# Convolution histories and taps loaded as rows of 32 channels and turned by VectorE; the first norm's scales loaded feature by feature

## The chip, the cores and the metric

The kernel runs on one core of a Trainium2 chip. A core has TensorE (PE; its weight loads are shown apart as PEld), VectorE (DVE), ScalarE (ACT), GpSimd (POOL) and SyncE (SP, which here only issues DMAs), and 16 DMA engines that all queues share. The metric is the device time of one execution in microseconds. The kernel before took 1661.09 us, the median of three runs (1659.3 to 1661.68).

## What is computed

One layer of a hybrid decoder for 256 new positions (the prompt) and 8 sequences of 4 positions (the samples), which continue from stored states. Cut to what bears on the change:

```python
proj = x @ w_in                                    # x: 288 rows of 2048 features
gB, gC, h, q, k, v, z, b_logit, a_logit, m_a, m_b = jnp.split(proj, split_points, axis=-1)
# convolutions along time, one per channel; the samples start from the last rows of their history
conv_out, new_conv_a = causal_depthwise_conv(gC * h, conv_a_buf, conv_a_w)            # 1024 channels, 3 taps, 2 rows
qkv, new_gdn_buf = causal_depthwise_conv(concat([q, k, v], -1), gdn_buf, gdn_conv_w)  # 3072 channels, 4 taps, 3 rows
...
o, S = gated_delta_rule(qh, kh, vh, g, beta, S0)
o = o * lax.rsqrt(jnp.mean(o * o, -1, keepdims=True) + NORM_EPS) * gdn_norm_w
...
x = layer_norm(ALPHA * x + merged @ w_o, ln1_g, ln1_b)
x = layer_norm(ALPHA * x + jnp.square(relu(x @ w_up)) @ w_down, ln2_g, ln2_b)
```

The inputs that the change concerns are the two histories (`state_gdn_conv`: 8 x 3 rows of 3072 channels; `state_conv_a`: 8 x 2 rows of 1024), the taps (`gdn_conv_w`: 4 rows of 3072; `conv_a_w`: 3 rows of 1024), the scales of the first layer norm (`ln1_g`, `ln1_b`: 2048 values each) and `gdn_norm_w` (128 values). In memory the channels are the fast index; the kernel wants channels on the 128 partitions.

## The kernel before

**Tiling.** Features stand on partitions, the 288 positions along the free dimension. Every large product runs over weight blocks of 512 KB, numbered from 0 in the order of the list `blocks`. Block i is loaded by SP into one of four buffers `raw` (`load(i)`, L177), split into a high part by ACT (`hi`, L187) and a low remainder by DVE (`lo`, L142), and used by 24 matmuls (L219 with `hi`, L221 with `lo`), which add into a PSUM accumulator `acc`. There are two accumulators, used in turn. A buffer `raw` is free again when DVE has made `lo`.

**The order of the work is written out by hand.** The main loop goes through the blocks; each turn of it puts instructions at the end of the queues of the engines, and each engine works its queue off in that order. Up to block 9 a turn i splits block i + 2 and, at its end, loads block i + 6. What a turn has for PE besides the matmuls stands in the list `fill` and is put between them, one entry after each second `lo` matmul. When a product is complete, its copies out of the accumulator are put into one of the next turns (`due`).

**The first blocks.** Blocks 0 to 3 serve the first two accumulators at once; blocks 4 to 7 finish them in turn, block 6 the first and block 7 the second. Block 8 begins the third product in the first accumulator, so it waits until turn 7's `conv_evac` (`pair`) has copied the first accumulator out (L277 and L279, ACT, two feature tiles). These copies go into the padded rows `w`, on which the convolution over time is done: ACT puts the samples' history in front (L278, from `hw`) and multiplies by the first tap (L281), DVE adds the other taps (L145).

**Histories and taps.** `hw` holds, for the 24 feature tiles of q, k and v, 24 columns of history and 4 of taps; `hwa` holds the same for the 8 tiles of the other convolution (16 and 3). `lnp` holds the scales of the first norm and `gdn_norm_w`. Before, SP loads the rows as they stand in memory into `hwr`, `har` and `lnr` (seven DMAs, behind the load of block 5). In turn 6 the entries `hist_tiles` and `hist_tiles2` of `fill` turn them by eleven PE transposes (L999, L1006 to L1008), and ACT copies the results out of PSUM (L1000, L1009, L1010, L1012). `gdn_norm_w` is used first when z is processed, `ln1_g` and `ln1_b` after that.

**DMAs on SP.** SP's and ACT's DMAs share eight completion semaphores in turn. An issue that takes up a semaphore again waits until the DMA that had it before, eight issues earlier, has landed; SP's later issues wait behind it.

**The middle.** From turn 8 on a generator (`side`) adds the work of the delta rule to the turns. Around turn 50, POOL and ACT copy the parts of `v3` (L1418 and L1416, `v<-hl`), from which ACT spreads `vm` (L1467) head by head.

Of the kernel before, what the change touches and what calls it, by code (L numbers as in the profile page):

```python
# [9 lines left out]
F32 = mybir.dt.float32  # L10
# [6 lines left out]
P = 128  # L17
# [88 lines left out]
def hybrid_kernel(ctx: ExitStack, tc: tile.TileContext, A):  # L106
# [31 lines left out]
    act, dve, pe, gps, sp = nc.scalar, nc.vector, nc.tensor, nc.gpsimd, nc.sync  # L138
# [22 lines left out]
    fill = []  # L161

    def at(i, f):
        due.setdefault(i, []).append(f)


    def load(i, steps=(), between=()):
        if i >= len(blocks):
            return
        gi, r0, k0, _, _ = blocks[i]  # L170
        t = wp.tile([P, KB, GW], F32, tag="raw", name=nm("raw"))
        kb, cols = gi["kb"], gi["cols"]
        dst = t.rearrange("p k c -> p (k c)").rearrange("p (k c) -> p k c", k=kb)
        src = gi["W"][r0:r0 + kb * P, gi["col0"]:gi["col0"] + cols].rearrange("(k p) c -> p k c", p=P)
        k = 0
        for step in steps or (kb,):
            sp.dma_start(dst[:, k:k + step], src[:, k:k + step])  # L177
            k += step
            if between:
                between.pop(0)()  # L180
        raw[i] = t
# [64 lines left out]
    ident = cst("ident")  # L246
# [630 lines left out]
    tx = tx_cm.__enter__()  # L877
# [12 lines left out]
    xsr = A["x_sample"].rearrange("b t (c j p) -> c (b t) j p", j=4, p=P)  # L890

    xtb, xm = (tx.tile([P, 1024], F32, name=n) for n in ("xtb", "xm"))
    hwr = tx.tile([112, 768], F32, name="hwr")
    har = tx.tile([76, 256], F32, name="har")
    lnr = tx.tile([33, P], F32, name="lnr")

    raw[0] = wp.tile([P, KB, GW], F32, tag="raw", name=nm("raw"))

# [3 lines left out]
    def x_sample_in(c, queue=sp):  # L902
        queue.dma_start(xs4[:, c * P:c * P + P], xsr[c])
# [15 lines left out]
    load(3)  # L919
    sp.dma_start(xr[2], xpr[:, :, 1024:1536])  # L920
    x_sample_in(2)
    gps.memset(epsc[:, 0:1], LN_EPS)
    gps.memset(epsc[:, 1:2], NORM_EPS)
    gps.memset(epsc[:, 2:3], 1.28e-10)

    def later_loads():
        sp.dma_start(xr[3], xpr[:, :, 1536:2048])
        x_sample_in(3)
        load(5)
        sp.dma_start(hwr[0:96, :], A["state_gdn_conv"][0].rearrange("b j (g c) -> (b j g) c", g=4))  # L930
        sp.dma_start(hwr[96:112, :], A["gdn_conv_w"][0].rearrange("j (g c) -> (j g) c", g=4))
        sp.dma_start(har[0:64, :], A["state_conv_a"][0].rearrange("b j (g c) -> (b j g) c", g=4))
        sp.dma_start(har[64:76, :], A["conv_a_w"][0].rearrange("j (g c) -> (j g) c", g=4))
        sp.dma_start(lnr[0:16, :], A["ln1_g"].rearrange("o (k p) -> (o k) p", p=P))
        sp.dma_start(lnr[16:32, :], A["ln1_b"].rearrange("o (k p) -> (o k) p", p=P))
        sp.dma_start(lnr[32:33, :], A["gdn_norm_w"])


    def x_sample(i):
# [52 lines left out]
            act.copy(xh[:, ks, 0:NP_], xv)  # L992
            tt(xl[:, ks, 0:NP_], xv, xh[:, ks, 0:NP_], SUB)

    def hist_tiles():
        g = gtile()
        hv = hw.rearrange("p (g u) c -> p u g c", u=6)
        for u in range(4):
            pe.transpose(g[:, u * 112:u * 112 + 112], hwr[:, u * P:(u + 1) * P], ident[0:112, 0:112])  # L999
        act.copy(hv[:, 0:4], g[:, 0:448].rearrange("p (u c g) -> p u g c", u=4, g=4))  # L1000

    def hist_tiles2():
        hv = hw.rearrange("p (g u) c -> p u g c", u=6)
        g2 = gtile()
        for u in range(2):
            pe.transpose(g2[:, u * 112:u * 112 + 112], hwr[:, (4 + u) * P:(5 + u) * P], ident[0:112, 0:112])  # L1006
            pe.transpose(g2[:, 224 + u * 76:300 + u * 76], har[:, u * P:(u + 1) * P], ident[0:76, 0:76])
        pe.transpose(g2[:, 376:409], lnr, ident[0:33, 0:33])  # L1008
        act.copy(hv[:, 4:6], g2[:, 0:224].rearrange("p (u c g) -> p u g c", u=2, g=4))  # L1009
        act.copy(hwa.rearrange("p (g u) c -> p u g c", u=2),  # L1010
                 g2[:, 224:376].rearrange("p (u c g) -> p u g c", u=2, g=4))
        act.copy(lnp, g2[:, 376:409])  # L1012


    G_ = {}
# [604 lines left out]
    idle = lambda: None  # L1620
# [23 lines left out]
    for i in range(len(blocks)):  # L1644
        cur[0] = i
        ahead = AHEAD if i > 9 else 2
        if i == 10:
            split_hi(i + 2)
            split_lo(i + 2)
        if i > 5:  # L1650
            split_hi(i + ahead)
        if i in (1, 3):
            a_, s_, b_ = x_fill(i // 2 + 1)
            fill.extend([idle, a_, s_, b_])
        if i == 5:
            fill.extend([idle, idle, lambda: x_sample(3)()])
        if i == 6:
            fill.extend([idle, idle, idle, idle, hist_tiles, hist_tiles2])
        if i == 7:
            tx_cm.__exit__(None, None, None)  # L1660
            gcm = tc.tile_pool(name="gdn", bufs=1)
            gpool = gcm.__enter__()
            gd["pool"] = gpool
            gd["w1"] = [gpool.tile([P, 640], F32, tag=f"w1{u}", name=f"w1{u}") for u in range(2)]
            for w in gd["w1"]:
                gps.memset(w[:, 0:3], 0.0)
            gps.memset(stBA, 0.0)
            for G in range(2):
                gd["kq", G] = gpool.tile([P, 4, 4, 2, 64], F32, tag="kq", name=f"kq{G}", bufs=2)
                gd["kqs", G] = gpool.tile([P, 2, 4, 8, 4], F32, tag="kqs", name=f"kqs{G}", bufs=2)  # L1670
                gd["v", G] = gpool.tile([P, 2, 4, 2, 64], F32, tag="vf", name=f"vf{G}")
                gd["vs", G] = gpool.tile([P, 4, 8, 4], F32, tag="vfs", name=f"vfs{G}")
        if i > 7 and sgen:
            if i == mark["merge"]:
                for _ in sgen:
                    pass
                sgen = None
            else:
                next(sgen, None)
                if aux and next(aux[0], aux) is aux:  # L1680
                    aux.pop(0)
            if i == mark["z"] + 4:
                states_out(24, 32, 2, 18, "vf", A["new_conv_a_prompt"][0, 0], A["new_conv_a_sample"][0])
            if i == mark["conv"] + 1:
                gd["ao"] = ap_.tile([P, 2, H, NT], F32, tag="ao", name="ao")
        late = i >= mark["end"] - 1
        if i > 5 and not late:
            split_lo(i + ahead)
        for f in due.pop(i, ()):
            f()  # L1690
        if late:
            split_lo(i + ahead)
        if i == mark["merge"]:
            gcm.__exit__(None, None, None)
            p3 = pool("p3")
            ph["pool"] = p3
            r1 = p3.tile([P, KT, NT], F32R, tag="R1", name="ahl")
            r4 = p3.tile([P, KT, NX], F32R, tag="R4", name="ohl")
            ph["mg"] = p3.tile([P, KT, NX], F32, tag="R3", name="mg")[:, :, 0:NT]

            def halves(key, r, src):
                for q in range(2):
                    s = slice(4 * q, 4 * q + 4)
                    s8 = slice(8 + 4 * q, 12 + 4 * q)
                    act.copy(r[:, s, 0:NT], src[:, s, :])
                    tt(r[:, s8, 0:NT], src[:, s, :], r[:, s, 0:NT], SUB)
                ph[key + "h"], ph[key + "l"] = r[:, 0:8, :], r[:, 8:16, :]

            halves("a", r1, gd["ao"][:, 0])
            at(i + 9, lambda: halves("o", r4, gd["ao"][:, 1]))  # L1710
        if i == mark["down3"]:
            tail_tiles()
        if i == mark["down3"] - 60:
            tail_consts()
        if i == mark["end"] - 3:
            sample_sum()
        if i == mark["end"] - 1:
            sample_products()
        matmuls(i)
        if i == 4:  # L1720
            x_last()
        if i < 6:
            for u, step in {0: ((1, 2),), 1: ((2, 1), (3, KB))}.get(i, ((i + 2, KB),)):
                split_hi(u, step)
                split_lo(u, step)
        if i == 2:
            x_turn()
# [41 lines left out]
```

## Time and profile before

| what | us |
|---|---|
| median of three runs | 1661.09 |
| lowest, highest | 1659.3, 1661.68 |
| the profiled execution | 1658.95 |
| its span from the first to the last instruction | 1656.8 |
| PE busy | 1648.6 |
| DVE busy | 981.2 |
| ACT busy | 785.8 |
| POOL busy | 138.8 |

The mean granted clock of TensorE in this execution is 0.999. Three views matter. The chain of waits follows the work that ended last back to what released it, step by step, and so tells which engine's time is the kernel's time. The timeline lists instructions by start and length (in us), with the engine, the line, the operation, what it writes and reads, and in brackets how long the engine stood idle before it and what ended that. The busy time by stretches tells how full each engine is in one part of the run. An "SPq" row is the issue of a DMA: its length is SP's time for the issue, and the landing comes later. L177, L187, L142, L219, L221 and L145 are lines of helpers that every block shares, so rows of different blocks read alike and are told apart by their start.

### The profile page before, as it was taken

The page shows a single profiled execution, that of the slowest core. Times are in us where ns is not written, and L with a number is a line of the kernel's source. Part 1 is how long each engine was busy: PE and PEld are TensorE (multiplying, and loading weights), DVE is VectorE, ACT ScalarE, POOL GpSimd, SP SyncE. Part 2 cuts the span into 40 slices and gives each one's busy share as a digit, 9 for nine tenths or more (in the row PEclk, how much of TensorE's full clock was granted, in tenths as well). Part 3 has the DMA queues.
Part 4 walks back from the last instruction along what each step waited for, and adds up shares of the span by engine and source line. Part 5 has one row for each costly group of instructions (what it writes and reads, how often), then busy time and mean ns, then how long its engine had stood idle before and what let it go on. Part 6 is the DMA issues. An engine that isn't in the chain of part 4 may idle for free.

```text
span 1656.8 us, 31402 instructions
## 1 busy us (share of the span) xinstructions
PE 1648.6 (100%) x13130; PEld 1634.0 (99%) x13130; DVE 981.2 (59%) x1299; ACT 785.8 (47%) x1231; POOL 138.8 (8%) x273
## 2 busy tenths in 40 slices
PE   9999999999999999999999999999999999999998
PEld 8999999999999999999999999999999999999997
DVE  6798678767544444457776666444444444444466
ACT  6786756448533333334444455443334433344354
POOL 1142216133000000000000000000000000000011
PEclk9999999999999999999999999999999999999999
DMA  8555457545555555554565555555555555555552
GB/s 272 176 169 172 135 173 203 184 130 175 185 170 165 166 165 165 166 166 157 167 217 164 166 166 166 166 166 166 165 166 166 166 166 165 166 166 166 180 162 100
DMA packets 273236, 280.42 MB, mean 169 GB/s; under 512 B 13727, under 2 KB 267220, under 8 KB 272832
## 3 DMA queue, kind: packets, MB, share of 16 engines
q1 hardware_dynamic: 269334, 266.33, 51.2%
q0 software_dynamic: 3616, 12.02, 2.6%
q8 instruction: 103, 1.69, 0.4%
q14 instruction: 39, 0.32, 0.1%
q10 hardware_dynamic: 144, 0.07, 0.0%
HBM read 270.88 MB, written 7.48 MB: 168 GB/s over the span
## 4 chain that ended last, share of the span: by engine, by line
PE 98%; DVE 1%; ACT 1%; DMA 0%; issue 0%; SPq 0%; ACTq 0%
PE acc L219 62%; PE acc L221 31%; PE acc L739 1%; PE g L1328 0%; PE g L1500 0%; PE g L1520 0%; PE g L1523 0%; DMA xr<-in_x_prompt_dram 0%; PE g L1319 0%; PE g L1220 0%; PE g L1478 0%; DVE lo L142 0%; PE g L1512 0%; DVE w L145 0%; DVE Y L145 0%
## 5 line engine op out<-in xcount | busy, mean ns | idle before, releaser
L142 DVE TENSOR_TENSOR lo<-raw,hi 128x1024 fp32r<-128x1024 f32 (+1 forms) x503 | 607.3, 1210 | 576.7 <-ACT hi L187 573.7
L187 ACT CAST hi<-raw 128x1024 fp32r<-128x1024 f32 (+1 forms) x499 | 519.1, 1043 | 729.5 <-PE acc L219 657.0
L219 PE MATMUL acc<-xh,hi 128*128 128x288 f32 x1408 | 397.9, 298 | 0.3 <-ACT xh L946 0.2
L219 PE MATMUL acc<-xl,hi 128*128 128x288 f32 x1408 | 394.2, 295 | 0.0
L221 PE MATMUL acc<-xh,lo 128*128 128x288 f32 x1408 | 302.6, 296 | 0.2 <-DVE lo L142 0.2
L219 PE MATMUL acc<-dl,hi 128*128 128x288 f32 (+1 forms) x1024 | 287.7, 295 | 0.0
L219 PE MATMUL acc<-dh,hi 128*128 128x288 f32 (+1 forms) x1024 | 287.4, 295 | 0.0
L219 PE MATMUL acc<-hl,hi 128*128 128x288 f32 x992 | 277.8, 295 | 0.0
L219 PE MATMUL acc<-hh,hi 128*128 128x288 f32 x992 | 277.4, 294 | 0.0
L219 PEld LDWEIGHTS acc<-xh,hi 128*128 128x128 f32 x1408 | 264.4, 188 | 3.1 <-issue 1.6
L219 PEld LDWEIGHTS acc<-xl,hi 128*128 128x128 f32 x1408 | 264.2, 188 | 1.1 <-DVE xl L142 0.3
L221 PEld LDWEIGHTS acc<-xh,lo 128*128 128x128 f32 x1408 | 226.0, 188 | 0.7 <-DVE lo L142 0.6
L221 PE MATMUL acc<-dh,lo 128*128 128x288 f32 (+1 forms) x1024 | 219.8, 296 | 0.0
L221 PE MATMUL acc<-hh,lo 128*128 128x288 f32 x992 | 213.2, 296 | 0.0
L219 PEld LDWEIGHTS acc<-dh,hi 128*128 128x128 f32 x1024 | 193.3, 189 | 0.0
L219 PEld LDWEIGHTS acc<-dl,hi 128*128 128x128 f32 x1024 | 192.8, 188 | 0.0
L219 PEld LDWEIGHTS acc<-hh,hi 128*128 128x128 f32 x992 | 186.4, 188 | 0.4 <-issue 0.4
L219 PEld LDWEIGHTS acc<-hl,hi 128*128 128x128 f32 x992 | 186.1, 188 | 0.0
L221 PEld LDWEIGHTS acc<-dh,lo 128*128 128x128 f32 x1024 | 164.5, 188 | 0.0
L221 PEld LDWEIGHTS acc<-hh,lo 128*128 128x128 f32 x992 | 159.0, 188 | 0.0
L219 PE MATMUL acc<-mh,hi 128*128 128x288 f32 x256 | 71.9, 297 | 0.0
L219 PE MATMUL acc<-ml,hi 128*128 128x288 f32 x256 | 71.7, 295 | 0.0
(423 smaller groups left out, 1489.1 us busy)
## 6 DMA issues: line engine op xcount, KB each, us to landing
raw<-in_w_in_dram SPq DMA_DIRECT2D x175, 512.0 KB, 3.5
raw<-in_w_up_dram SPq DMA_DIRECT2D x128, 512.0 KB, 3.6
raw<-in_w_down_dram SPq DMA_DIRECT2D x128, 512.0 KB, 3.6
raw<-in_w_o_dram SPq DMA_DIRECT2D x32, 512.0 KB, 3.7
raw<-in_w_a_out_dram SPq DMA_DIRECT2D x16, 512.0 KB, 3.6
raw<-in_w_b_out_dram SPq DMA_DIRECT2D x16, 512.0 KB, 3.6
S<-in_state_gdn_dram POOLq DMA_DIRECT2D x8, 512.0 KB, 5.5
out_dram<-S POOLq DMA_DIRECT2D x8, 512.0 KB, 4.7
```

Source lines behind the costliest of these rows:

```text
L142: dve.tensor_tensor(out=out, in0=a, in1=b, op=op)
L187: act.copy(his[i][:, k:k + step], raw[i][:, k:k + step])
L219: pe.matmul(o, h[:, k, c], x, start=st and x is xh_, stop=False)
L221: pe.matmul(o, l[:, k, c], xh_, start=False, stop=en)
L739: pe.matmul(out, x[:, kk, c], w[:, k, :], start=False, stop=stop)
```

## The change

The seven loads of `hwr`, `har` and `lnr` and the eleven PE transposes go, with the ACT copies out of PSUM. In their place:

- `hist_in` issues sixteen DMAs on SP at the end of turn 1, behind the load of block 7 and ahead of that of block 8. Four for each of the four tensors, one for each group q of 32 partitions: row r of a tensor goes to partition 32 q + r (+ an offset), as pieces of 32 channels, one per feature tile. The taps stand behind the histories in the same group. POOL fills the tile `hb` with zeros at the start.
- `hist_turn`, at the end of turn 6, is one DVE transpose of the whole tile by squares of 32 x 32, `hbt` from `hb`, after which channel 32 q + f stands on its partition; two ACT copies bring `hw` and `hwa` into place.
- `norm_in`, at the end of turn 50, issues three DMAs on POOL that bring `ln1_g`, `ln1_b` and `gdn_norm_w` straight into `lnp`, one value of four bytes at a time.

```diff
-    hwr = tx.tile([112, 768], F32, name="hwr")
-    har = tx.tile([76, 256], F32, name="har")
-    lnr = tx.tile([33, P], F32, name="lnr")
+    hb, hbt = (tx.tile([P, 32, 32], F32, name=n) for n in ("hb", "hbt"))
...
+    gps.memset(hb, 0.0)
     gps.memset(epsc[:, 0:1], LN_EPS)
...
         load(5)
-        sp.dma_start(hwr[0:96, :], A["state_gdn_conv"][0].rearrange("b j (g c) -> (b j g) c", g=4))
-        sp.dma_start(hwr[96:112, :], A["gdn_conv_w"][0].rearrange("j (g c) -> (j g) c", g=4))
-        sp.dma_start(har[0:64, :], A["state_conv_a"][0].rearrange("b j (g c) -> (b j g) c", g=4))
-        sp.dma_start(har[64:76, :], A["conv_a_w"][0].rearrange("j (g c) -> (j g) c", g=4))
-        sp.dma_start(lnr[0:16, :], A["ln1_g"].rearrange("o (k p) -> (o k) p", p=P))
-        sp.dma_start(lnr[16:32, :], A["ln1_b"].rearrange("o (k p) -> (o k) p", p=P))
-        sp.dma_start(lnr[32:33, :], A["gdn_norm_w"])
+
+    def hist_in():
+        for t0, r0, src in ((0, 0, A["state_gdn_conv"][0].rearrange("b j c -> (b j) c")), (0, 24, A["gdn_conv_w"][0]),
+                            (24, 0, A["state_conv_a"][0].rearrange("b j c -> (b j) c")), (24, 16, A["conv_a_w"][0])):
+            n, c = src.shape
+            for q in range(4):
+                sp.dma_start(hb[32 * q + r0:32 * q + r0 + n, t0:t0 + c // P],
+                             src.rearrange("r (t q f) -> q r t f", q=4, f=32)[q])
+
+    def norm_in():
+        for u, n in enumerate(("ln1_g", "ln1_b")):
+            gps.dma_start(lnp[:, 16 * u:16 * u + 16], A[n].rearrange("o (k p) -> p (o k)", p=P))
+        gps.dma_start(lnp[:, 32:33], A["gdn_norm_w"].rearrange("o p -> p o"))
...
-    def hist_tiles():
...
-    def hist_tiles2():
...
+    def hist_turn():
+        dve.transpose(out=hbt.rearrange("p t c -> p (t c)"), in_=hb.rearrange("p t c -> p (t c)"))
+        act.copy(hw, hbt[:, 0:24, 0:28])
+        act.copy(hwa, hbt[:, 24:32, 0:19])
...
-        if i == 6:
-            fill.extend([idle, idle, idle, idle, hist_tiles, hist_tiles2])
...
         load(i + ahead + 4)
+        if i == 1:
+            hist_in()
+        if i == 6:
+            hist_turn()
+        if i == 50:
+            norm_in()
```

More of the change, by code (lines that the diff above doesn't have):

```diff
@@ L993, in x_last @@
             tt(xl[:, ks, 0:NP_], xv, xh[:, ks, 0:NP_], SUB)
-    def hist_tiles():
[L996 to L1000, printed above, removed]
-    def hist_tiles2():
[L1003 to L1012, printed above, removed]
+    def hist_turn():
+        dve.transpose(out=hbt.rearrange("p t c -> p (t c)"), in_=hb.rearrange("p t c -> p (t c)"))
+        act.copy(hw, hbt[:, 0:24, 0:28])
+        act.copy(hwa, hbt[:, 24:32, 0:19])
     G_ = {}
```

## The prediction

> **What bounds the kernel now.** I read the page's busy table, then its chain of waits, then the busy time by stretches around the place of the change.
>
> ```profile
> PE 1648.6 (100%) x13130; PEld 1634.0 (99%) x13130; DVE 981.2 (59%) x1299; ACT 785.8 (47%) x1231; POOL 138.8 (8%) x273
> PE 98%; DVE 1%; ACT 1%; DMA 0%; issue 0%; SPq 0%; ACTq 0%
> ...
> 20.00:28.00 8.00, 8.00 (x63) 8.00 (x62) 4.87 (x7) 7.22 (x14) 4.57 (x10) 1.00 0.80 260
> 28.00:36.00 8.00, 8.00 (x62) 7.75 (x61) 5.09 (x8) 5.49 (x18) 1.02 (x3) 1.00 0.81 268
> 36.00:60.00 24.00, 24.00 (x198) 22.70 (x197) 22.45 (x28) 17.85 (x47) 0.00 (x0) 1.00 0.70 200
> ```
>
> PE carries 98% of the chain, and it has no idle time in the stretches around the edit and behind it (columns: PE, PEld, DVE, ACT and POOL busy, granted clock, DMA share, GB/s). So the change is worth what it takes from PE's queue, less any new wait of PE. What other engines save counts only through such a wait.
>
> **What is removed from PE.** Eleven transposes stand inside block 6 (blocks are counted from 0; 24 matmuls each).
>
> ```profile
> 30.54 0.29 PE L219 MATMUL acc<-xl,hi 128*128 128x288 f32 x1
> 30.67 0.30 PE L221 MATMUL acc<-xh,lo 128*128 128x288 f32 x1
> 30.80 0.55 PE L999 MATMUL g<-cf,hwr 112*128 112x112 f32 x4
> 31.12 0.38 PE L221 MATMUL acc<-xh,lo 128*128 128x288 f32 x1
> ...
> 31.77 0.24 PE L1008 MATMUL g<-cf,lnr 33*128 33x33 f32 x1
> 31.94 0.40 PE L219 MATMUL acc<-xh,hi 128*128 128x288 f32 x1
> 32.18 0.29 PE L219 MATMUL acc<-xl,hi 128*128 128x288 f32 x1
> ...
> 36.02 0.29 PE L219 MATMUL acc<-xh,hi 128*128 128x288 f32 x1
> ```
>
> Undisturbed matmuls start 0.13 us apart (30.54 to 30.67). From 30.67 to 32.18 there are three steps, 0.39 us by that pitch, and 1.51 us passed: the transposes cost **1.1 us** of PE, all of it on the path. Block 8, which starts at 36.02, would start at 34.9.
>
> **What must be ready by then.** Block 8 is the first to reuse the first accumulator, so PE must wait there until ACT has copied block 6's result out. In the changed kernel, more stands ahead of those copies. ACT's queue before (`hi_438` is weight block 8, `hi_484` is block 9, `w_490` the first copy out of the accumulator):
>
> ```order
> L187 CAST hi_438<-raw_312 128x1024
> L1000 COPY hw<-g_459 128x4x4x28
> L1009 COPY hw<-g_466 128x2x4x28
> L1010 COPY hwa<-g_466 128x2x4x19
> L1012 COPY lnp<-g_466 128x33
> L187 CAST hi_484<-raw_366 128x1024
> L277 COPY w_490<-acc_163 128x256
> ```
>
> and now, where `hi_447` and `hi_481` are the same blocks 8 and 9:
>
> ```order
> L187 CAST hi_447<-raw_321 128x1024
> L1003 COPY hw<-hbt 128x672
> L1004 COPY hwa<-hbt 128x152
> L187 CAST hi_481<-raw_375 128x1024
> L277 COPY w_487<-acc_156 128x256
> ```
>
> The copies of the histories used to wait for PE; now they read `hbt`, which DVE writes in its turn, and DVE's turn stands behind the `lo` half of block 8. So everything hangs on the landing of block 8's weights. I call its time L.
>
> ```profile
> 28.08 1.05 ACT L187 CAST hi<-raw 128x1024 fp32r<-128x1024 f32 x1
> 29.58 1.22 DVE L142 TENSOR_TENSOR lo<-raw,hi 128x1024 fp32r<-128x1024 f32 x1
> 18.44 1.24 DVE L980 STREAM_TRANSPOSE xtb<-xr 128x1024 f32<-128x1024 f32 x1
> 31.39 0.53 ACT L1000 COPY hw<-g 128x448 f32<-128x448 f32 x1 [2.26 <-PE g L999]
> 32.05 0.35 ACT L1009 COPY hw<-g 128x224 f32<-128x224 f32 x1
> 32.29 0.30 ACT L1010 COPY hwa<-g 128x152 f32<-128x152 f32 x1
> 32.54 1.07 ACT L187 CAST hi<-raw 128x1024 fp32r<-128x1024 f32 x1
> 33.49 0.39 ACT L277 COPY w<-acc 128x256 f32<-128x256 f32 x1
> 35.13 0.19 ACT L279 COPY w<-acc 128x32 f32<-128x32 f32 x1
> ```
>
> The new chain, term by term: `hi` of block 8 1.05 (28.08), `lo` 1.22 (29.58), DVE's turn 1.24 (the row at 18.44 has the same shape), the copy of `hw`, `hwa`, `hi` of block 9, then the copies out of the accumulator. The `hw` copy now has 672 elements in one piece; 448 took 0.53 and 224 took 0.35, so 0.8 ns an element more gives 0.71. ACT's instructions overlap by 0.1 us (hi at 32.54 lasts 1.07, its successor starts after 0.95), so I count 0.61, 0.20 and 0.95. From 33.49 to 35.13 + 0.19 = 35.32 the copies out take 1.83. With 0.15 for hand-overs between engines (estimate from the 0.07 between the end of the turn at 19.68 and POOL's start at 19.75, below), the sum is 1.05 + 1.22 + 1.24 + 0.61 + 0.20 + 0.95 + 1.83 + 0.15 = 7.25. Block 8 cannot start before L + 7.25, and it would like to start at 34.9: PE stalls for L − 27.65, if that is positive. Before, the copies out ended at 35.32, 0.7 us ahead of block 8; that cover is used up by the turn. What is late next: ACT and DVE then run 0.7 us closer behind PE; from 36 to 60 ACT has 6 us free and DVE 1.5, so they should make it up with no second stall.
>
> **When block 8's weights land.** On SP's queue, before (`raw_154` is block 5, `raw_312` block 8):
>
> ```order
> L177 DMA raw_154<-in_w_in_dram 128x4x256
> L930 DMA hwr<-in_state_gdn_conv_dram 96x768
> L931 DMA hwr<-in_gdn_conv_w_dram 16x768
> L932 DMA har<-in_state_conv_a_dram 64x256
> L933 DMA har<-in_conv_a_w_dram 12x256
> L934 DMA lnr<-in_ln_g_dram 16x128
> L935 DMA lnr<-in_ln_b_dram 16x128
> L936 DMA lnr<-in_gdn_norm_w_dram 1x128
> L177 DMA raw_213<-in_w_in_dram 128x4x256
> L177 DMA raw_271<-in_w_in_dram 128x4x256
> L177 DMA raw_312<-in_w_in_dram 128x4x256
> ```
>
> and now (`raw_206`, `raw_264`, `raw_321` are blocks 6, 7, 8):
>
> ```order
> L177 DMA raw_154<-in_w_in_dram 128x4x256
> L177 DMA raw_206<-in_w_in_dram 128x4x256
> L177 DMA raw_264<-in_w_in_dram 128x4x256
> L936 DMA hb<-in_state_gdn_conv_dram 24x24x32 x4
> L936 DMA hb<-in_gdn_conv_w_dram 4x24x32 x4
> L936 DMA hb<-in_state_conv_a_dram 16x8x32 x4
> L936 DMA hb<-in_conv_a_w_dram 3x8x32 x4
> L177 DMA raw_321<-in_w_in_dram 128x4x256
> ```
>
> Seven issues ahead of blocks 6 to 8 become sixteen, between blocks 7 and 8.
>
> ```profile
> 11.85 0.51 SPq L930 DMA_DIRECT2D hwr<-in_state_gdn_conv_dram  x1
> ...
> 15.01 0.60 SPq L933 DMA_DIRECT2D har<-in_conv_a_w_dram  x1
> ...
> 17.89 0.28 SPq L936 DMA_DIRECT2D lnr<-in_gdn_norm_w_dram  x1
> 19.84 0.40 SPq L177 DMA_DIRECT2D raw<-in_w_in_dram  x1
> ...
> 21.34 0.46 SPq L177 DMA_DIRECT2D raw<-in_w_in_dram  x1
> 15.99 1.22 DVE L142 TENSOR_TENSOR lo<-raw,hi 128x1024 fp32r<-128x1024 f32 x1
> 21.00:27.50 6.50, 6.50 (x51) 6.50 (x50) 3.64 (x5) 6.02 (x13) 3.65 (x8) 1.00 0.94 307
> raw<-in_w_in_dram SPq DMA_DIRECT2D x175, 512.0 KB, 3.5
> r<-in_ln_g_dram SPq DMA_DIRECT2D x1, 8.0 KB, 3.9
> ```
>
> Block 7's load needs the buffer that the `lo` at 15.99 frees at 17.21; SP is free again near 17.65, and the sixteen begin. An issue takes 0.28 to 0.60 us here, 0.41 in the mean of the seven, plus some 0.05 to the next: 0.46. The queue holds eight DMAs at once, each issue waiting for the landing of the one eight before it (that is why the seven are spread over 11.85 to 17.89, and why block 6 was issued only at 19.84, when block 5 had landed). So the ninth of the sixteen waits for the first. That one lies behind blocks 6 and 7: block 5 landed at about 19.8, and at 307 GB/s a block of 512 KB takes 1.7 us, so they land near 21.5 and 23.2 and the first history near 23.5. Then eight issues of 0.46 are left, and block 8 is issued at 27.2 instead of 21.34. In a queue that is then quiet it lands 3.5 us later: L = 30.7, a stall of 3.05 us, and **the sum −1.1 + 3.05 = +1.9 us**.
>
> Bounds: with 0.33 an issue and no wait for a landing the sixteen end at 22.9, L = 26.4, no stall, −1.1. With 0.65 an issue block 8 goes at 28.7, and if it took the 6.7 us that lay between its issue at 21.34 and its `hi` at 28.08 before, L = 35.4 and the sum is +6.6. The true value should be nearer to the 3.5, since the queue has nothing else large in it. The histories themselves come in 3,296 pieces of 128 bytes; the row of 3.9 us is a load of 2,048 pieces of four bytes, so the last one, issued at 26.7, lands near 30.6. DVE reaches its turn at L + 2.3 = 33.0: hidden, with 2.4 us of cover.
>
> The Trainium skill, "DMA: Bandwidth & Descriptors", section "Rules for kernel authors", speaks against the edit: transfers under 64 KB pay mostly overhead and should be merged. Its section on the anatomy of one DMA puts the fixed part at about 2.0 us; sixteen in series would be 32 us by that estimate. The seven rows above go out within 6 us and so overlap; the trace does not bear that sum out.
>
> **The rest.**
>
> ```profile
> 19.75 0.39 POOL L987 COPY xm<-xtb 32x256 f32<-32x256 f32 x1 [18.33 <-DVE xtb L980]
> 74.10 1.04 POOL L1130 DMA_DIRECT2D S<-in_state_gdn_dram  x1
> 192.93 0.97 POOL L1418 CAST v<-hl 32x128 fp32r<-32x128 f32 x3
> 204.16 2.45 ACT L1467 ACTIVATE vm<-v,cf 128x128 fp32r<-128x128 f32 x8
> 207.28 1.05 ACT L187 CAST hi<-raw 128x1024 fp32r<-128x1024 f32 x1 [0.67 <-PE acc L219]
> L145 DVE SCALAR_TENSOR_TENSOR ao<-sz,lnp,ao x4: 811/816/993, 381.5 to 421.1; 128x576 f32<-128x576 f32 x4
> ```
>
> The fill of `hb` costs POOL about 1 us (its three fills in the stretch 28 to 36, one of the same 128x1024, took 1.02) and lies in 18.33 us of idle time: nothing. The three loads of the norm's scales stand on POOL's queue in the middle of the copies into `v` that end at 192.93 + 0.97 = 193.9. A load of 1,024 pieces took 1.04 us to issue; twice that for 2,048 pieces, two of them and a small one make 2.5 to 5 us, and the copies end by 199. The ACT work on their heads is the third set of `vm`, behind the `hi` at 207.28: 9 us of cover or more. The scales are used first at 381.5. ACT's three copies of the histories, 1.18 us, become two of 1.01; nothing waits for the difference.
>
> **The rivals.** (A) Late: SP is held up longer, L above 32, and the kernel is slower by more than 0.2%. For it:
>
> ```profile
> 31.25 0.52 SPq L1633 DMA_DIRECT2D ao<-in_w_in_dram  x1
> 34.90 3.47 SPq L177 DMA_DIRECT2D raw<-in_w_in_dram  x1
> ```
>
> An issue behind a load of 2,048 pieces took 3.47 us, where the one at 19.84 took 0.40. If that befalls block 8, add 3.1: +5.0, 1666.1. It decides from L = 32.1, one and a half microseconds above my sum. (B) Covered: L below 28.8, the stall at most the gain, 1660.0 to 1661.1; against it stand sixteen issues at the measured lengths. (C) POOL: the loads of the scales take several times my price, the third set of `vm` waits, and ACT's later `hi` with it. To reach 208 the issues must last 14 us, three times my upper bound; beyond that each microsecond counts. With 20 us it is +6 on top of the sum, 1669. The Trainium skill, "SBUF — State Buffer", on DMAs from GpSimd, says VectorE can lock GpSimd out of writing descriptors (620 ns becoming 3100); that fivefold would be about 24 us. The 1.04 us row, with VectorE busy on and off, does not show it. (D) Series, as in the rule above: sixteen loads at 3.9 us one behind another, over 30 us slower. (E) A gain above 0.2%: only 1.1 us is taken from PE, so it has no mechanism.
>
> **How the numbers follow.** The profiled execution took 1658.95 us, 0.13% under the median of the runs, 1661.09; I add the sum to the median: 1663.0. 0.2% (3.3 us) is about what a measurement of this kernel can tell from no change. Chances: my case, +0 to +3.3, 0.46; A 0.33; B 0.08; C 0.08; D 0.01; E 0.04. Slower is A, C and D: 0.42; same is my case and B: 0.54; faster 0.04. The range runs from B's best, a little below 1660, to beyond A's, 1668.5; my own case alone is 1661 to 1664.4.
>
> **What the changed profile would show.** No transposes at 30.8; block 8's load issued near 27 and landed near 31; its `hi` idle before it for 2 to 3 us on that DMA; DVE's turn right behind its `lo`; one PE gap of about 3 us at the first matmul of block 8, released by ACT's copy out of the accumulator, and none near 200 us. If that gap is missing or doubled, the length of the sixteen issues was wrong; if PE waits elsewhere, so was the reading.

## The result, and the profile after

The changed kernel takes 1668.74 us (median of 4 runs, 1667.17 to 1669.24); on the same chip the kernel before takes 1660.88 us. The ratio is 1.0050, with a 95% interval of 1.0038 to 1.0063: it is slower by about 7.9 us. The forecast was 1663.0, at most 1668.5. The profiled execution took 1667.17 us with a span of 1665.3, against 1658.95 and 1656.8 before; the spans differ by 8.5.

From the page of the changed kernel, PE's busy time, the chain by engine, and the one group of matmuls with idle time ahead of it:

```profile
PE 1649.3 (99%) x13121; PEld 1634.7 (98%) x13121; DVE 982.0 (59%) x1300; ACT 785.7 (47%) x1229; POOL 142.8 (9%) x277
...
PE 96%; DVE 1%; SPq 1%; ACT 1%; DMA 1%; issue 0%; ACTq 0%
...
L219 PE MATMUL acc<-xh,hi 128*128 128x288 f32 x1408 | 399.0, 299 | 8.1 <-ACT w L279 7.9
```

SP's queue and DMA, at 0% of the chain before, now hold 1% each, and PE waits once, for 7.9 us, on ACT's copy out of the accumulator. The count of matmuls falls by nine, from 13,130 to 13,121: the transposes that go are nine, not the eleven that the texts above name. The same view by stretches as in the prediction, with three finer ones (PE, PEld, DVE, ACT, POOL busy, granted clock, DMA share, GB/s):

```profile
20.00:28.00 8.00, 8.00 (x63) 8.00 (x62) 4.86 (x7) 7.23 (x14) 4.58 (x10) 1.00 0.46 98
28.00:36.00 8.00, 7.11 (x53) 6.81 (x52) 1.68 (x3) 0.40 (x2) 0.00 (x0) 1.00 0.39 116
36.00:60.00 24.00, 17.04 (x117) 17.04 (x118) 20.86 (x25) 18.05 (x46) 1.02 (x3) 0.86 0.75 229
40.00:43.00 3.00, 0.04 (x1) 0.04 (x1) 1.73 (x3) 2.87 (x12) 1.02 (x3) 0.50 1.07 373
43.00:46.00 3.00, 3.00 (x12) 3.00 (x13) 2.89 (x6) 2.97 (x5) 0.00 (x0) 0.50 1.04 191
46.00:47.00 1.00, 1.00 (x8) 1.00 (x8) 1.00 (x2) 1.00 (x6) 0.00 (x0) 0.90 0.81 251
```

Two things are to be seen. From 20 to 36, where the kernel before moved 260 GB/s and more, the DMA engines are busy for less than half of the time: no further weight block was asked of them. And when PE works again at 43, its granted clock is 0.50: 12 matmuls in three microseconds. In the kernel before the same stretch reads:

```profile
43.00:46.00 3.00, 3.00 (x25) 3.00 (x24) 2.93 (x5) 1.86 (x4) 0.00 (x0) 1.00 0.26 70
```

SP's queue of the changed kernel (start, length over all instructions of the row, line, tile, count), then what the DMA engines moved from 23.0 to 32.2 us:

```profile
15.92 1.74 SPq L177 DMA_DIRECT2D raw<-in_w_in_dram  x2
17.75 5.97 SPq L936 DMA_DIRECT2D hb<-in_state_gdn_conv_dram  x4
23.76 2.70 SPq L936 DMA_DIRECT2D hb<-in_gdn_conv_w_dram  x4
26.51 2.54 SPq L936 DMA_DIRECT2D hb<-in_state_conv_a_dram  x4
29.09 3.07 SPq L936 DMA_DIRECT2D hb<-in_conv_a_w_dram  x4
32.26 1.16 SPq L177 DMA_DIRECT2D raw<-in_w_in_dram  x2
...
DMA packets 2318, 0.30 MB, mean 33 GB/s; under 512 B 2312, under 2 KB 2317, under 8 KB 2317
```

The sixteen issues go on without a wait between them from 17.75 to 32.16, 14.4 us, with the DMA engines at 33 GB/s. Only then is the load of block 8 issued, at 32.26 instead of 21.34. What follows from it on ACT, DVE and PE:

```profile
34.68 0.43 PE L221 MATMUL acc<-xh,lo 128*128 128x288 f32 x2
35.80 1.04 ACT L187 CAST hi<-raw 128x1024 fp32r<-128x1024 f32 x1 [7.60 <-DMA raw<-in_w_in_dram]
36.88 1.22 DVE L142 TENSOR_TENSOR lo<-raw,hi 128x1024 fp32r<-128x1024 f32 x1 [7.20 <-ACT hi L187]
38.02 1.24 DVE L1002 STREAM_TRANSPOSE hbt<-hb 128x1024 f32<-128x1024 f32 x1
39.29 0.75 ACT L1003 COPY hw<-hbt 128x672 f32<-128x672 f32 x1 [2.45 <-DVE hbt L1002]
40.17 1.04 ACT L187 CAST hi<-raw 128x1024 fp32r<-128x1024 f32 x1
42.72 0.19 ACT L279 COPY w<-acc 128x32 f32<-128x32 f32 x1
42.96 0.61 PE L219 MATMUL acc<-xh,hi 128*128 128x288 f32 x1 [7.85 <-ACT w L279]
43.60 0.44 PE L219 MATMUL acc<-xh,hi 128*128 128x288 f32 x1
43.84 0.44 PE L219 MATMUL acc<-xl,hi 128*128 128x288 f32 x1
...
47.69 0.29 PE L219 MATMUL acc<-xh,hi 128*128 128x288 f32 x1
```

The last row is the first matmul of block 9; before, it was

```profile
39.21 0.29 PE L219 MATMUL acc<-xh,hi 128*128 128x288 f32 x1
```

PE issued the last matmul of block 7 at 34.81 (the second of the two at 34.68) and would have gone on at 34.94, 1.1 us earlier than before; the two executions start block 1 within 0.04 us of each other (10.13 and 10.17), so their positions can be compared. Block 8 starts at 42.96: 8.0 us late. Then its matmuls start 0.24 us apart instead of 0.13, so that block 9 starts 4.73 us behind block 8 (47.69 to 42.96) instead of 3.19 (39.21 to 36.02 before): 1.5 us more. The sum −1.1 + 8.0 + 1.5 = 8.4 is the difference of the spans, 8.5. Behind that nothing is lost.

### The profile page after: what moved, and what is told of

The parts are those of the page before. It is cut to its first block, busy times and chain, and to the rows that moved or that the text cites. A ratio compares the mean times of both kernels' runs of the same rounds, so it can differ in the third digit from the quotient of the medians.

```text
span 1665.3 us, 31402 instructions
## 1 busy us (share of the span) xinstructions
PE 1649.3 (99%) x13121; PEld 1634.7 (98%) x13121; DVE 982.0 (59%) x1300; ACT 785.7 (47%) x1229; POOL 142.8 (9%) x277
## 4 chain that ended last, share of the span: by engine, by line
PE 96%; DVE 1%; SPq 1%; ACT 1%; DMA 1%; issue 0%; ACTq 0%
PE acc L219 61%; PE acc L221 31%; SPq L936 1%; PE acc L739 1%; DMA cf<-in_cf_dram 0%; ACT hi L187 0%; PE g L1320 0%; PE g L1492 0%; PE g L1512 0%; PE g L1515 0%; DVE lo L142 0%; DMA xr<-in_x_prompt_dram 0%; PE g L1311 0%; PE g L1212 0%; PE g L1470 0%
```

## The experiments

Three theories stood. *SP's queue*: the sixteen issues hold up block 8's load, all else follows. *The turn*: DVE's turn and the copies behind it are late by themselves. *The scales*: part comes from their loads on POOL. And of the slow matmuls behind the stall it had to be told whether PE's idle time causes them. One caution for all times: block 1 starts between 10.1 and 12.8 us in these profiles, and the kernel before itself ranges over some 3 us. Two things make the start uneven: PE's waits for the first inputs, up to 1.55 us each, and the pace of the first matmuls, which start 0.24 us apart instead of 0.13, in some executions until 8 to 11 us, in others (the kernel before, the changed one) until about 5. In the last version below, which has no such wait, the slow pace lasts until 9.35 and block 1 starts at 11.47. Positions are therefore compared within one trace, from block 1 on.

### Without the loads

```diff
-        if i == 1:
-            hist_in()
```

> The changed kernel without its sixteen loads of the histories and taps; the fill with zeros, DVE's turn, the two copies and the loads of the norm's scales stay, so what is left out is the histories and taps themselves (they are zero). Theory 1 (SP's queue: the sixteen issues hold up the load of block 8): the load of block 8 is issued by 21 us, its hi is not late, block 8's first matmul starts at 34.9 with no stall, and the kernel is 1.1 us faster than before, near 1659.8 us, ratio 0.9993. Theory 2 (the turn on DVE and the bigger copies on ACT are late by themselves, whatever the loads do): a stall of 1 to 3 us stays at block 8, near 1662. Theory 3 (part of the 7.9 us comes from the loads of the norm's scales on POOL): 1 to 2 us stay, somewhere behind 190 us.

Measured: 1660.48 us, ratio 1.0000 (0.9992 to 1.0009).

```profile
29.34 2.00 ACT L187 CAST hi<-raw 128x1024 fp32r<-128x1024 f32 x2
37.87 0.40 PE L219 MATMUL acc<-xh,hi 128*128 128x288 f32 x1 [0.57 <-ACT w L279]
```

The loads make nearly the whole stall: 0.57 us stay of 7.85. But these stay: the turn has a small share. Here `hi` of block 8 is the second of the two at 29.34, back to back with that of block 7, so it is ACT's own queue and no landing that starts the chain, and the chain ends 0.6 us after PE is ready. (The histories and taps are left out of this kernel, so its results are not those of the layer.)

### The two parts of the change

```diff
-        sp.dma_start(lnr[0:16, :], A["ln1_g"].rearrange("o (k p) -> (o k) p", p=P))
-        sp.dma_start(lnr[16:32, :], A["ln1_b"].rearrange("o (k p) -> (o k) p", p=P))
-        sp.dma_start(lnr[32:33, :], A["gdn_norm_w"])
...
-        pe.transpose(g2[:, 376:409], lnr, ident[0:33, 0:33])
...
-        act.copy(lnp, g2[:, 376:409])
...
+        if i == 50:
+            norm_in()
```

> The kernel before with the second part of the change alone: the norm's scales are loaded by POOL after block 50, and their three early loads, their transpose on PE and their copy on ACT are gone; the histories go the old way. My theory: one transpose less, about 0.2 us, three SP issues less in a place where SP had time, and POOL's loads hidden: 1660.7, the same. Rival: the loads on POOL hold up the copies into v and the third set of vm near 208 us: 1 us or more slower, with a stall near 200 to 210.

Measured: 1659.78 us, ratio 0.9999 (0.9990 to 1.0008), and PE waits nowhere near 200 us. The scales cost nothing. The changed kernel's own trace says the same: POOL's queue with the three loads, and the stretch around them.

```profile
200.98 1.16 POOL L941 DMA_DIRECT2D lnp<-in_ln_g_dram  x1
202.13 1.15 POOL L941 DMA_DIRECT2D lnp<-in_ln_b_dram  x1
203.27 0.56 POOL L942 DMA_DIRECT2D lnp<-in_gdn_norm_w_dram  x1
...
190.00:230.00 40.00, 40.00 (x311) 39.26 (x310) 29.95 (x64) 26.85 (x71) 9.07 (x16) 1.00 0.51 144
```

They hold POOL for 2.87 us, and PE is busy for all 40 us.

### Fewer loads: how the stall follows the queue, and the clock the stall

With eight loads (those of both taps left out):

```diff
-        for t0, r0, src in ((0, 0, A["state_gdn_conv"][0].rearrange("b j c -> (b j) c")), (0, 24, A["gdn_conv_w"][0]),
-                            (24, 0, A["state_conv_a"][0].rearrange("b j c -> (b j) c")), (24, 16, A["conv_a_w"][0])):
+        for t0, r0, src in ((0, 0, A["state_gdn_conv"][0].rearrange("b j c -> (b j) c")),
+                            (24, 0, A["state_conv_a"][0].rearrange("b j c -> (b j) c"))):
```

> The changed kernel with eight loads instead of sixteen: those of the taps (the two weights) are left out, so the taps are zero; the four of 576 pieces and the four of 128 stay. SP's queue as the cause: 17.75 + 5.9 for the first four + 4 x 0.67 = 26.4 for the issue of block 8's load; landing 3.5 us later at 29.9; plus 7.2 makes 37.1 for block 8's first matmul against 34.9: a stall of about 2.2 us, and with -1.1 a time 1.1 us over that of before, 1662.0. On the clock: after the stall of 8 us PE's granted clock fell to 0.5 for about 3 us; if that needs a stall longer than about 3.4 us, it stays at 1.00 here; if any stall does it, 1.5 us more, 1663.5. If the turn and not the queue were the cause, the stall would stay near 8 us.

With twelve (the four of `gdn_conv_w` left out):

```diff
-        for t0, r0, src in ((0, 0, A["state_gdn_conv"][0].rearrange("b j c -> (b j) c")), (0, 24, A["gdn_conv_w"][0]),
-                            (24, 0, A["state_conv_a"][0].rearrange("b j c -> (b j) c")), (24, 16, A["conv_a_w"][0])):
+        for t0, r0, src in ((0, 0, A["state_gdn_conv"][0].rearrange("b j c -> (b j) c")),
+                            (24, 0, A["state_conv_a"][0].rearrange("b j c -> (b j) c")), (24, 16, A["conv_a_w"][0])):
```

> The changed kernel with twelve loads: the four of the first tap's weights are left out, so those taps are zero. Between the eight (a stall of 1.4 us, clock at 1.00 behind it) and the sixteen (7.9 us, 0.5). By SP's queue: four issues of 0.68 less than sixteen, so block 8's load goes 2.7 us earlier, near 29.5, and the stall is about 5 us; it tells whether 5 us of idle time cost the clock. If they do, 1.5 to 2.5 us come on top: 1660.5 - 1.1 + 5 + 2 = 1666.4; if not, 1664.4.

Eight loads took 1659.67 us, ratio 0.9997 (0.9988 to 1.0006); the first four went out in 4.93 us instead of 5.9, so the stall is 1.35 us and not 2.2. Twelve took 1665.73, ratio 1.0036 (1.0023 to 1.0048), with a stall of 3.9 us and the low clock. They stand with two later experiments in one table. The second column is the time from block 1's first matmul to the issue of block 8's load, which takes the start's variation out.

| kernel | issue of block 8's load after block 1 | PE idle ahead of block 8 | block 8 to block 9 | clock behind the idle time | median |
|---|---|---|---|---|---|
| no loads | 8.25 | 0.57 | 3.28 | 1.00 | 1660.48 |
| eight | 15.21 | 1.35 | 3.29 | 1.00 | 1659.67 |
| sixteen, whole rows | 17.79 | 3.45 | 4.56 | 0.50 | 1662.93 |
| twelve | 17.84 | 3.88 | 4.79 | 0.50 | 1665.73 |
| sixteen, small ones first | 19.67 | 5.9 | 5.44 | 0.50 | 1667.19 |
| changed kernel | 22.09 | 7.85 | 4.73 | 0.50 | 1668.74 |

From eight loads on, the idle time is the issue time less 13.8 to 14.3 in every row: the landing and the chain behind it take the same time, and the issue on SP's queue alone sets the stall. The turn, which all of them contain, is excluded as the cause of more than the first row's 0.57. In this table the clock is at 0.50 behind 3.45 us of idle time and more, and stays at 1.00 behind 1.35 us; the halved stretch costs 1.3 to 2.2 us, by the fourth column against its first row. Twelve loads came out slower than the times would have it (1665.73 where −1.1 + 4.0 + 1.6 on 1660.0 gives 1664.5); the start of its profiled run was 1.5 us late, and more than that I can't say.

### PE kept busy in the stall

```diff
+        if i == 8:
+            wps = gtile()
+            warm_up(32)
         matmuls(i)
```

(`warm` moves to a pool that is still open there.)

> The changed kernel with 32 matmuls of 128x512 in bf16 on zeros put into PE's queue ahead of block 8, 0.215 us each at full clock, 6.9 us of the 8 us in which it waits there; nothing uses their result. If the clock fell to 0.5 because PE was idle for 8 us: it stays at 1.00, block 9 starts 3.2 us behind block 8 instead of 4.7, and the kernel takes about 1.5 us less than the changed one, 1667.2. If the slow matmuls behind the stall have another reason (late weights, ACT or DVE behind), block 9 still starts 4.7 us behind block 8 and the time is that of the changed kernel.

Measured: 1666.01 us, ratio to the kernel before 1.0038 (1.0024 to 1.0052) where the changed kernel has 1.0050. PE's timeline and two stretches:

```profile
35.32 7.08 PE L884 MATMUL g<-warm 128*128 128x512 bf16 x32
43.23 0.40 PE L219 MATMUL acc<-xh,hi 128*128 128x288 f32 x1 [0.83 <-ACT w L279]
...
36.00:43.00 7.00, 6.40 (x30) 2.71 (x28) 3.87 (x4) 4.39 (x12) 1.02 (x3) 1.00 1.05 365
43.00:46.00 3.00, 2.77 (x21) 2.77 (x22) 2.86 (x7) 2.95 (x6) 0.00 (x0) 1.00 0.80 140
```

Block 8 starts as late as ever, but the clock is 1.00 throughout, 21 matmuls run from 43 to 46 instead of 12, and block 9 follows after 3.29 us. So the slow matmuls came from PE's idle time, not from ACT or DVE. The two intervals overlap; it is the trace that decides this. The Trainium skill, "TensorE: Matmul & The Clock Gate", section "Part 1: The HAM clock gate", says that one idle window of about 3.4 us halves PE's clock and that about 3.4 us of work restore it. The stalls at blocks 6 and 8 agree: 0.50 behind 3.43 us and more, 1.00 behind 1.35, and some 3 us at the low clock in the changed kernel (2.8 to 4.8 in the others). But the clock also fell once behind a shorter wait: in the profile of the spread version below it is 0.50 from 8 to 11 us, behind a wait of 1.55 us for the first inputs, with PE busy for 0.45 us of the two from 6 to 8. So these runs do not fix a limit.

### Which of the sixteen are slow to issue

```diff
-        for t0, r0, src in ((0, 0, A["state_gdn_conv"][0].rearrange("b j c -> (b j) c")), (0, 24, A["gdn_conv_w"][0]),
-                            (24, 0, A["state_conv_a"][0].rearrange("b j c -> (b j) c")), (24, 16, A["conv_a_w"][0])):
+        for t0, r0, src in ((24, 16, A["conv_a_w"][0]), (24, 0, A["state_conv_a"][0].rearrange("b j c -> (b j) c")),
+                            (0, 24, A["gdn_conv_w"][0]), (0, 0, A["state_gdn_conv"][0].rearrange("b j c -> (b j) c"))):
```

> The changed kernel with the four groups of loads in the reverse order: the 24-piece ones first, the 576-piece ones last. Three theories of why the first four issues took 0.96 to 2.28 us and the rest 0.59 to 0.77. Place (they stood behind the loads of blocks 6 and 7 in a full queue): now the first four small ones take 1 to 2.3 us and the last four, of 576 pieces, about 0.7; the sixteen again take 14 us. Pieces (576 pieces take longer to issue anywhere): the first twelve take 0.6 to 0.77, the last four 1 to 2.3 us each; again 14 us. Both needed (many pieces and a full queue): all sixteen take 0.6 to 0.77, 11 us in all; block 8's load goes at 29 instead of 32.26, the stall falls from 8 to about 5 us, and the kernel takes about 1665. By the first two the time is that of the changed kernel, 1668.7.

```profile
19.06 3.24 SPq L936 DMA_DIRECT2D hb<-in_conv_a_w_dram  x4
...
24.95 2.75 SPq L936 DMA_DIRECT2D hb<-in_gdn_conv_w_dram  x4
27.73 3.30 SPq L936 DMA_DIRECT2D hb<-in_state_gdn_conv_dram  x4
```

The four loads of 576 pieces take 3.30 us at the end of the queue, 5.97 behind the loads of blocks 6 and 7; the small ones are as long as there, to 0.2. So the many pieces alone do not make an issue of 0.96 to 2.28 us; the place behind the large loads is needed too. It does something by itself: the longest small one in that place takes 0.90, and of the whole rows below one takes 1.36 there. The sixteen take 12.0 us: 2.4 less, and the stall falls from 7.85 to 5.9. The prediction of that case, 11 us and a stall of 5, was near; its time of 1665 was not (1667.19, ratio 1.0042, 1.0030 to 1.0055), since the clock was low for over 4 us here.

Then the same sixteen loads as whole rows, one piece of 3,072 or 1,024 bytes instead of 24 or 8 of 128:

```diff
-                sp.dma_start(hb[32 * q + r0:32 * q + r0 + n, t0:t0 + c // P],
-                             src.rearrange("r (t q f) -> q r t f", q=4, f=32)[q])
+                sp.dma_start(hb[32 * q + r0:32 * q + r0 + n].rearrange("p t f -> p (t f)")[:, 32 * t0:32 * t0 + c // 4],
+                             src[:, q * (c // 4):(q + 1) * (c // 4)])
```

> The changed kernel with its sixteen loads in the same place of SP's queue and with the same bytes, but each row read as one piece of 3,072 or 1,024 bytes instead of 24 or 8 pieces of 128; the elements then stand in the wrong places of the histories. If the number of pieces makes an issue long: they take about 0.41 each as the row-shaped loads of the kernel before did, the sixteen end near 25, block 8's load goes 7 us earlier than in the changed kernel, and the stall falls to 0.7 to 1.5 us with the clock at 1.00: 1660.0 to 1661.0. If an issue costs 0.6 whatever the pieces: block 8's load goes near 28, the stall is about 3.5 us and the clock falls: 1664.

SP's queue, the single issues of one kind (count; shortest, median, longest in ns; first and last start), and SP's waits from 17 to 28:

```profile
17.64 2.65 SPq L936 DMA_DIRECT2D hb<-in_state_gdn_conv_dram  x4
20.33 4.39 SPq L936 DMA_DIRECT2D hb<-in_gdn_conv_w_dram  x4
24.77 1.70 SPq L936 DMA_DIRECT2D hb<-in_state_conv_a_dram  x4
26.51 1.24 SPq L936 DMA_DIRECT2D hb<-in_conv_a_w_dram  x4
27.85 1.49 SPq L177 DMA_DIRECT2D raw<-in_w_in_dram  x3
...
L936 SPq DMA_DIRECT2D hb<-in_gdn_conv_w_dram x4: 248/270/295, 20.3 to 24.5; - x4
...
SPq L936 <- DMA raw<-in_w_in_dram: 3.2, 2, 1.9
```

Measured: 1662.93 us, ratio 1.0014 (1.0005 to 1.0023), between the two forecasts, with a stall of 3.45 us. Its executions range from 1660.59 to 1664.76, wider than those of the kernel before (1659.0 to 1661.78); whether the clock stays up in some of them, the one trace does not show. An issue is as short as I had taken it, 0.25 to 0.47 apart from one of 1.36, where in 128-byte pieces the same loads took 0.59 and more. But now the queue's limit shows: the seventh and the eighth issue wait 3.2 us for the landings of blocks 6 and 7, which the expectation had left out. With slow issues that wait is hidden, with short ones it is not. Block 8's load goes at 27.85.

### The loads in other places

Three versions look for what the change could give. First, SP's issues where SP waits for buffers anyway: five behind block 5's load, four behind block 8's, seven behind block 9's.

```diff
         load(5)
+        hist_in(5)
...
-        if i == 1:
-            hist_in()
+        if i in (2, 3):
+            hist_in(4 if i == 2 else 7)
```

> The changed kernel with the same sixteen loads in the places where SP's queue sat waiting for buffers: five behind block 5's load, four behind block 8's, seven behind block 9's. If the order on SP's queue is the cause: block 8's load is issued by about 21 us, its hi is not late, and the stall of 8 us at block 8 falls to the 0.6 us that also stood in the kernel without the sixteen loads (there the chain through DVE's turn ended that much late); with -1.1 the kernel is 0.5 us faster than before, 1660.0. If 3,296 pieces of 128 bytes cost time of their own (DMA engines kept from the weights), a stall stays at block 9 or 10, 2 us or more, and the time is above 1662.

Measured: 1661.15 us, ratio 1.0006 (0.9997 to 1.0015); PE idle for 0.60 us ahead of block 8, as without the loads, and behind it, up to 150 us, only for the 0.2 to 0.3 us near 125 us that the other traces have too. The time is 1.15 us above the forecast; in its profile, 2.4 us longer in span than that of the kernel before, block 1 starts 2.6 us later (12.71 against 10.13), before the first of the sixteen loads is issued at 14.47. The same sixteen loads of the same pieces, and 7.3 us of the stall are gone: their place in SP's queue was the cause.

Next, POOL's queue at the start of the program:

```diff
-                sp.dma_start(hb[32 * q + r0:32 * q + r0 + n, t0:t0 + c // P],
+                gps.dma_start(hb[32 * q + r0:32 * q + r0 + n, t0:t0 + c // P],
...
         load(5)
+        hist_in()
...
-        if i == 1:
-            hist_in()
```

> The changed kernel with the sixteen loads issued by POOL at the start, ahead of its copies into xm, instead of by SP. If SP's queue is what they cost: block 8's load goes by 21 us and the stall is the 0.6 to 0.8 us of the kernel without loads, 1660.0 to 1660.5. Against it: they then move while the first weights and inputs fill the DMA engines (from 5 to 20 us those are busy throughout), 412 KB at about 380 GB/s are 1.1 us more there, and 3,296 pieces of 128 bytes may take several times that: PE's first blocks start later, 1661 to 1664. If POOL needs over 1 us for an issue, its copies into xm at 19.75 us are late too and PE waits near 25 us.

Measured: 1663.92 us, ratio 1.0022 (1.0013 to 1.0031). PE's waits from 7 to 45 us (in all, times, longest):

```profile
PE g L964 <- DMA xr<-in_x_prompt_dram: 2.5, 2, 1.5
PE acc L219 <- DVE xl L142: 0.9, 1, 0.9
PE acc L219 <- ACT hi L187: 0.7, 1, 0.7
PE acc L219 <- ACT w L279: 0.6, 1, 0.6
```

At block 8 PE is idle for 0.6 us only, but the first inputs and what hangs on them are late. From 10 to 20 us the DMA engines are as busy as in the kernel before (share 1.10 against 1.04) but move 275 GB/s instead of 343: the pieces compete with the loads of the start. The stall is traded for others, 4.7 us in these rows.

Then DVE's turn ahead of the `lo` of block 7:

```diff
+        hist_in(6)
...
+        if i == 2:
+            hist_in(10)
+        if i == 4:
+            dve.transpose(out=hbt.rearrange("p t c -> p (t c)"), in_=hb.rearrange("p t c -> p (t c)"))
```

> The sixteen loads on SP as six behind block 5's load and ten behind block 8's, and DVE's turn between the lo of block 6 and the lo of block 7 instead of behind the lo of block 8; ACT's copies stay where they were. If the 0.6 us left without the loads come from the turn standing on the chain hi, lo, turn, copy, hi, copies out: no stall at block 8, the whole 1.1 us are gained, 1659.4. If the histories land too late for DVE (after 28.3 us), lo of block 7 is late and PE waits up to 1 us at block 7 instead: 1660.4.

```profile
32.21 1.25 DVE L1732 STREAM_TRANSPOSE hbt<-hb 128x1024 f32<-128x1024 f32 x1 [2.38 <-DMA hb<-in_gdn_conv_w_dram]
33.69 0.60 PE L219 MATMUL acc<-xl,hi 128*128 128x288 f32 x1 [3.43 <-DVE xl L142]
34.00:37.00 3.00, 3.00 (x14) 3.00 (x14) 3.00 (x3) 1.42 (x3) 1.02 (x3) 0.50 0.89 274
```

Measured: 1664.47 us, ratio 1.0027 (1.0017 to 1.0038), worse than either forecast. The turn waits 2.4 us for the last history, and in DVE's queue behind it stands an `xl` that PE needs in block 6: 3.4 us of idle time, and the clock falls again. I had counted the `lo` behind the turn, not the `xl`.

### A version that takes the gain

In the spread version, ACT's copies of the histories move behind the `hi` of block 9:

```diff
         if i == 7:
+            hist_copies()
```

> The kernel with the sixteen loads spread over SP's free places, and ACT's two copies of the histories moved behind the hi of block 9 (before: ahead of it); DVE's turn stays behind the lo of block 8. If the 0.6 to 0.8 us left at block 8 come from that hi waiting behind the copies, which wait for the turn: the chain is 0.95 us shorter, no stall at block 8, and the whole 1.1 us are gained: 1659.0 to 1659.4, 0.07% under the kernel before, within what can be measured. If the copies out of the accumulator wait for the turn anyway, 0.3 us or more of the stall stay.

Measured: 1660.15 us, ratio 0.9999 (0.9990 to 1.0008), with PE idle for 0.93 us ahead of block 8, where none had been forecast. DVE's timeline names the next link:

```profile
32.67 1.25 DVE L1008 STREAM_TRANSPOSE hbt<-hb 128x1024 f32<-128x1024 f32 x1 [1.05 <-DMA hb<-in_gdn_conv_w_dram]
```

The turn waits for the last history, issued by SP at 29.97. So three of the sixteen go to POOL, behind its copies into `xm`:

```diff
             x_moves(gps.tensor_copy, range(10))
+            hist_in(3, gps)
...
-            hist_in(4 if i == 2 else 7)
+            hist_in(4)
```

> As the kernel with the spread loads and the late copies, but three of the sixteen loads are issued by POOL behind its copies into xm (where POOL is idle and the DMA engines are half empty), so that SP's last one goes 2 us earlier. There the turn on DVE sat idle for 1.1 us on the last history, issued near 30, and PE waited 0.9 us at block 8. If that landing was the last link: the turn follows the lo of block 8 without a gap, no stall of PE at block 8, the whole 1.1 us of the removed transposes are gained: 1659.2, 0.07% under the kernel before and too little to tell from it by the times alone; the trace shows it by the absence of the gap. If POOL's loads land later than SP's did (POOL's issues for the histories took 0.5 to 0.9 us, and landed 5 us and more later while the DMA engines were full), the gap stays.

Measured: 1658.89 us (1658.08 to 1660.73, 11 runs) against 1659.96, ratio 0.9994 (0.9985 to 1.0003).

```profile
32.02 1.24 DVE L1008 STREAM_TRANSPOSE hbt<-hb 128x1024 f32<-128x1024 f32 x1
36.26 0.32 PE L219 MATMUL acc<-xh,hi 128*128 128x288 f32 x1
34.00:38.00 4.00, 4.00 (x33) 4.00 (x31) 2.70 (x6) 3.82 (x14) 1.02 (x3) 1.00 1.01 345
```

The turn follows without a gap and PE never stops. From block 1's first matmul to block 8's are 24.79 us, against 25.89 in the kernel before: the 1.1 us are there in the trace. The times agree, but the interval includes no change. It is 0.6% under the changed kernel as given.

## Why the prediction was wrong

The direction and the chain held, the size did not.

- **The transposes, −1.1 us.** Right: PE was ready for block 8 at 34.94 (forecast 34.9), and the last version keeps the gain. Their number was wrong, nine and not eleven; the 1.1 us were read from the timeline and do not hang on it.
- **From landing to block 8, 7.25 us.** Right: 42.96 − 35.80 = 7.16. The 3.5 us from issue to landing too: 32.26 to 35.80.
- **Sixteen issues at 0.46 us, block 8's load issued at 27.2. This step failed.** They took 14.4 us, 0.90 each, and the load went at 32.26: 5 us late, which is 5 us of stall. (The prediction's own sign for this, a gap that is doubled, came true: 7.85 us for about 3.) The price came from seven rows of the kernel before, whose pieces are 512 to 3,072 bytes long; the changed loads come in 128-byte pieces. As whole rows, sixteen issues in the same place end at 27.8, with waits for landings as forecast (though for blocks 6 and 7, which I had not counted among the eight), and that kernel takes 1662.93 us. In pieces, each issue is longer by 0.2 to 0.5 and the first four by up to 2. The changed shape was in the prediction (it counts 3,296 pieces); it was used for the landing and not for the issue.
- **The wait of the ninth issue.** Did not bind: the issues were so slow that the landings kept up.
- **The clock.** A missing term of 1.5 us: each stall of 3.45 us and more at block 8 cost 1.3 to 2.2 us on top. Rival A, whose stall comes to 6.1 us, would have needed it.
- **Rival A** named the place, SP held longer, and was given 0.33. Its row, an issue of 3.47 us, did not befall block 8's load (0.40 in the trace); the time went in the sixteen themselves. With their true length and the clock the rival's sum is −1.1 + 8.0 + 1.5.
- **The stall is L − 27.65.** It has a floor that I left out: ACT reached the `hi` of block 8 at 28.08 even with the weights there, so 0.4 us were always left by that formula, and 0.57 were measured without loads. In this order of the queues, covered (rival B) was never worth the full 1.1.
- **POOL and the scales, nothing; no second stall.** Right: 2.87 us in the bounds of 2.5 to 5, and rival C did not occur.
- **Rival D**, the loads in series, did not occur: SP issued the sixteen in 14.4 us without a wait. The 2.0 us that the prediction took from the Trainium skill, "DMA: Bandwidth & Descriptors", section "Anatomy of one DMA — SWDGE (gpsimd) path", are stated there for DMAs issued by GpSimd; these were issued by SP.

The time lies 0.2 us beyond the range, because the range's upper case combined a late load with an undisturbed clock. That case came close to the landing, L = 35.4 against 35.80, but by another road, an issue at 28.7 and a landing 6.7 us later; so that the time is so near the range is in part luck.

## What to carry to other kernels

Price a DMA for its issuing queue by its shape, and take the price from a row of that shape: a layout that saves work on an engine can move it into a queue, where it delays whatever stands behind. Before placing a run of small loads, look for what the queue must issue next and for where the queue itself waits; with the same sixteen loads PE stood idle for 7.9 us in one place and for 0.6 in another. Where a stall of PE can reach some 3 us, add what the clock loses behind it: 1.3 to 2.2 us here.

## What the runs showed of the hardware

- An issue on SP took longer in 128-byte pieces than as whole rows of the same bytes, and not in proportion to the pieces: 0.63 to 0.66 us against 0.25 to 0.29 (96 pieces), 0.59 to 0.62 against 0.32 to 0.42 (128), 0.71 to 0.77 against 0.26 to 0.30 (24). With 576 pieces it was 0.78 to 0.81 at the end of the run of loads and 0.80 to 2.42 behind two or three loads of 512 KB. What holds those up, a limit on pieces in flight or something else, was not told apart.
- While SP issued such loads for 9 us, the DMA engines moved 33 GB/s.
- PE's granted clock fell to 0.50 after idle times of 3.43, 3.45, 3.88, 5.9 and 7.85 us, not after 1.35 at block 8, and stayed there for some 3 to 5 us of work; it began to fall 2.9 to 4.3 us after PE's last matmul (worked out from the mean clock of stretches of 1 us). Once it fell behind a wait of 1.55 us, near 8 us in the spread version. Matmuls on zeros in bf16 kept it at 1.00.
